# Joining the in-chunk products of a chunked scan: one pinned run for four chunks instead of one group for two

## Chip, cores and metric

The kernel runs on one core of a Trainium2 chip. The metric is the device time of one execution in microseconds (us). Engines: TensorE (PE, with its weight loads as PEld), VectorE (DVE), ScalarE (ACT), GpSimd (POOL) and SyncE (SP), which issues the DMAs here. Each engine works through its own row of instructions in order and waits at semaphores for the others.

## The reference

One layer of a hybrid backbone on 1024 latent and 128 context tokens (1152 rows, 1024 columns, f32). The change lies in the bidirectional Mamba-2 scan. With 128-token chunks, for each of 32 heads and for each direction:

```
L      = exp(where(mask, a_cs[i] - a_cs[j], -inf))
y_diag = (C B^T * L) @ x                      # inside a chunk
states = B^T (decay * x)                      # of each chunk
h      = dec * h + states                     # chain over the chunks
y_off  = C (exp(a_cs) * h_prev)               # from the chunks before
y      = y_f + flip(y_b) + D * x
```

Around it stand an input projection, a depthwise convolution with SiLU ahead of x, B and C, an output gate z, and a gated norm; behind it a gMLP branch, the merge, and a ConvFFN.

## The kernel before

The projection (names `gps`, L301 to L303) is written as 72 products of 128x384 per 128 output columns: three split-precision products for eight row blocks and three token blocks. Such a set of 72 is called a unit here. They fill TensorE's row between the small products of the scan. Their PSUM tiles have three buffers, and a unit's results go on through ACT (L356 to `pad` for x, B and C, L592 to `z`) before its next blocks can reuse a bank.

The scan works on 16 pairs of heads (q = 0 to 15), four pairs to a group that shares B and C. Chunks are taken in steps: s = 0 to 3 are two latent chunks each, s = 4 is the context chunk. For a pair:

- `ssd_loads(q, s)` (L632) loads R, the running sums broadcast for the decay matrix; for s < 4 E (tile EP), the exponents for the part from earlier chunks; for s = 4 H, the starting state.
- `mstage(s)` (L662) turns R into the masked decay matrix: biases on ACT (L672) and DVE (L674), a limit (L677), the exponentials on ACT (L678, and E's on L680), the product with C B^T (L688), and the sum of both directions, written back into R (L689).
- `chain(s)` (L697) carries the state on: weighted x (`xwf`, `xwb`, L694), products `pst` (L709, L710) in one PSUM bank, and steps of H on DVE (L713, L715).
- `ctx_state` (L717) makes the final context state in the same bank (`pstc`, L724).
- `main(s)` (L729) makes the output: the products `yo` (L740) with the state, the products `yd` (L744) inside the chunk, and on DVE L749 to L752 (L754 for the context). `yd` multiplies 128x64 halves: the two heads of a pair go to two halves of the array.

Steps are handed out between the units by `merge`. A scheduler then fixes each engine's row from its own model of time, with the scan's steps at a raised priority (P_SCAN). So the row of an engine isn't the order of the code, and the whole row may change where dependencies change. `queue_behind` (L274) is the way to pin one instruction directly after another in that order. At the end of a unit, `ptX` and `ptB` (L549) transpose x and B, after the convolution on DVE (L541, L542, L528).

Of the kernel before, what the change touches and what calls it, by code (L numbers as in the profile page):

```python
# [4 lines left out]
F32 = mybir.dt.float32  # L5
# [41 lines left out]
def gcol(t):  # L47
    return t if t < NL else t + 1
# [60 lines left out]
def body(tc, A, O):  # L109
# [517 lines left out]
    def cc_of(s):  # L627
        return [2 * s, 2 * s + 1] if s < 4 else [8]

    Rt, EPt, Ht = {}, {}, {}  # L630

    def ssd_loads(q, s):  # L632

        cc = cc_of(s)
        n = len(cc)
        R = spa.p.tile([128, 2, 2, 2, 128], F32, tag="R", name=f"R{q}{s}", bufs=3)
        if n == 2:
            SP.dma_start(R.rearrange("p d h c i -> p (d h) (c i)"),
                         acs_scr[q, :, :, cc[0]:cc[0] + 2].rearrange("d h c i -> (d h) (c i)").unsqueeze(0).to_broadcast([128, 4, 256]))
        else:  # L640
            SP.dma_start(R[:, :, :, 0, :].rearrange("p d h i -> p (d h) i"),
                         acs_scr[q, :, :, cc[0]].rearrange("d h i -> (d h) i").unsqueeze(0).to_broadcast([128, 4, 128]))
        Rt[q, s] = R
        if s < 4:
            E = spa.p.tile([128, 2, 2, 128], F32, tag="EP", name=f"EP{q}{s}", bufs=2)
            for h in range(2):
                SP.dma_start(E[64 * h:64 * h + 64].rearrange("p d c i -> p d (c i)"),
                             acs_scr[q, :, h, cc[0]:cc[0] + 2].rearrange("d c i -> d (c i)").unsqueeze(0).to_broadcast([64, 2, 256]))
            EPt[q, s] = E
        if s == 4:  # L650
            H = spa.p.tile([128, 8, 2, 128], F32, tag="H", name=f"H{q}", bufs=2)
            SP.dma_start(H[:, 0], A["h0"][q])
            Ht[q] = H

    def ssd(q):

        g = q // 4
        _, Bt, CT, CB = groups[g]
        X, Xt = xq[q]
        Dc = par[:, P_D + q:P_D + q + 1]  # L660

        def mstage(s):  # L662
            cc = cc_of(s)
            n = len(cc)
            R = Rt[q, s]
            for d in range(2):
                for h in range(2):
                    col = 32 * d + 2 * q + h
                    for i, c in enumerate(cc):
                        r = R[:, d, h, i, :]  # L670
                        if 4 * d + 2 * h + i < NACT:
                            S.activation(r, r, AF.Identity, bias=nb[:, c, col:col + 1])  # L672
                        else:
                            V.tensor_scalar(r, r, nb[:, c, col:col + 1], 60.0, op0=ALU.add, op1=ALU.min)  # L674
            Rv = R.rearrange("p d h c i -> p (d h) c i")[:, :, :n]
            if NACT:
                V.tensor_scalar(Rv[:, :NACT // 2], Rv[:, :NACT // 2], 60.0, None, op0=ALU.min)  # L677
            S.activation(Rv, Rv, AF.Exp)  # L678
            if s < 4:
                S.activation(EPt[q, s], EPt[q, s], AF.Exp)  # L680
            for d in range(2):
                if n == 2:
                    r = R[:, d].rearrange("p h c i -> p h (c i)")
                    cb = CB[:, d, cc[0]:cc[0] + 2, :].rearrange("p c i -> p (c i)").unsqueeze(1).to_broadcast([128, 2, 256])
                else:
                    r = R[:, d, :, 0, :]
                    cb = CB[:, d, cc[0], :].unsqueeze(1).to_broadcast([128, 2, 128])
                V.tensor_tensor(r, r, cb, op=ALU.mult)  # L688
            V.tensor_tensor(R[:, 0, :, :n], R[:, 0, :, :n], R[:, 1, :, :n], op=ALU.add)  # L689

        def xw(c0, n, d, dst):

            wv = wst[:, c0:c0 + n, 32 * d + 2 * q:32 * d + 2 * q + 2].unsqueeze(3).to_broadcast([128, n, 2, 64])
            V.tensor_tensor(dst.rearrange("p c (h e) -> p c h e", h=2), Xt[:, c0:c0 + n].rearrange("p c (h e) -> p c h e", h=2),  # L694
                            wv, op=ALU.mult)

        def chain(s):  # L697

            H = Ht[q]
            ks = [2 * s, 2 * s + 1] if s < 3 else [6]  # L700
            n = len(ks)
            x0 = spa.p.tile([128, 2, 128], F32, tag="xwf", name=f"xwf{q}{s}", bufs=2)[:, :n]
            x1 = spa.p.tile([128, 2, 128], F32, tag="xwb", name=f"xwb{q}{s}", bufs=2)[:, :n]
            xw(ks[0], n, 0, x0)
            cb0 = 7 - ks[-1]
            xw(cb0, n, 1, x1)
            ps = pst.tile([128, 2, 2, 128], F32, tag="st", name=f"pst{q}{s}")
            for i, k in enumerate(ks):
                PE.matmul(ps[:, i, 0, :], lhsT=Bt[:, k, :], rhs=x0[:, i, :], start=True, stop=True)  # L709
                PE.matmul(ps[:, i, 1, :], lhsT=Bt[:, 7 - k, :], rhs=x1[:, 7 - k - cb0, :], start=True, stop=True)  # L710
            for i, k in enumerate(ks):
                cd = cdk[:, k, :, 2 * q:2 * q + 2].unsqueeze(3).to_broadcast([128, 2, 2, 64])
                V.tensor_tensor(H[:, k + 1].rearrange("p d (h e) -> p d h e", h=2), H[:, k].rearrange("p d (h e) -> p d h e", h=2),  # L713
                                cd, op=ALU.mult)
                V.tensor_tensor(H[:, k + 1], H[:, k + 1], ps[:, i], op=ALU.add)  # L715

        def ctx_state():  # L717
            x0 = spa.p.tile([128, 2, 128], F32, tag="xwf", name=f"xwc{q}", bufs=2)
            for d in range(2):
                xw(8, 1, d, x0[:, d:d + 1])  # L720
            ps = pst.tile([128, 2, 2, 128], F32, tag="st", name=f"pstc{q}")
            so = spa.p.tile([128, 2, 128], F32, tag="so", name=f"so{q}")
            for d in range(2):
                PE.matmul(ps[:, 0, d, :], lhsT=x0[:, d, :], rhs=Bt[:, 8, :], start=True, stop=True)  # L724
            S.copy(so, ps[:, 0])
            for d in range(2):
                SP.dma_start(O[2 + d][0, 0, 2 * q:2 * q + 2].rearrange("h p n -> (h p) n"), so[:, d, :])

        def main(s):  # L729
            cc = cc_of(s)  # L730
            n = len(cc)
            R = Rt.pop((q, s))
            o = gcol(128 * cc[0])
            if s < 4:
                H = Ht[q]
                yo = pyo.tile([128, 2, 2, 128], F32, tag="yo", name=f"yo{q}{s}")
                for i, c in enumerate(cc):
                    for d in range(2):
                        k = c if d == 0 else 7 - c
                        PE.matmul(yo[:, d, i, :], lhsT=H[:, k, d, :], rhs=CT[:, 128 * c:128 * c + 128], start=True, stop=True)  # L740
            yd = pyd.tile([128, 512], F32, tag="yd", name=f"yd{q}{s}")[:, :128 * n]
            for i, c in enumerate(cc):
                for h in range(2):
                    PE.matmul(yd[64 * h:64 * h + 64, 128 * i:128 * i + 128], lhsT=Xt[:, c, 64 * h:64 * h + 64],  # L744
                              rhs=R[:, 0, h, i, :], start=True, stop=True, tile_position=(0, 64 * h))
            xv = X[:, o:o + 128 * n]
            if s < 4:
                E = EPt.pop((q, s))
                V.tensor_tensor(E, E, yo, op=ALU.mult)  # L749
                V.scalar_tensor_tensor(xv, xv, Dc, E[:, 0].rearrange("p c i -> p (c i)"), op0=ALU.mult, op1=ALU.add)  # L750
                V.tensor_tensor(xv, xv, E[:, 1].rearrange("p c i -> p (c i)"), op=ALU.add)
                V.tensor_tensor(xv, xv, yd, op=ALU.add)  # L752
            else:
                V.scalar_tensor_tensor(xv, xv, Dc, yd, op0=ALU.mult, op1=ALU.add)  # L754

        def nxt(s):
            if q + 1 < 16:
                ssd_loads(q + 1, s)

        def step(*fs):  # L760
            def run():
                for f, *a in fs:
                    f(*a)
            return run
        pro = [step((mstage, 4), (chain, 0)), step((mstage, 0), (chain, 1)), step((chain, 2)), step((chain, 3))]
        outs = [step((mstage, 1), (main, 4), (ssd_loads, q, 2)), step((mstage, 2), (main, 0), (ssd_loads, q, 3), (ctx_state,)),
                step((mstage, 3), (main, 1), (nxt, 4)), step((main, 2), (nxt, 0)), step((main, 3), (nxt, 1))]
        return pro, outs

    def merge(fills, steps):  # L770
# [35 lines left out]
    gtp.p, gtp.bufs = spa.p, 1  # L806
    run_unit(first_x)
    for s in (4, 0, 1):
        ssd_loads(0, s)
    after = None  # L810
    for q in range(17):
        steps = []
# [523 lines left out]
```

## Time and profile before

| what | value |
|---|---|
| median of 3 runs | 2480.05 us (2478.02 to 2480.44) |
| the profiled execution | 2481.27 us |
| its span | 2479.3 us |
| granted TensorE clock, mean | 0.994 |
| PE / DVE / ACT busy, share of the span | 98% / 75% / 45% |
| scan, first `yo` to last DVE step | about 134 to 958 us of the span |

Busy times count an instruction from its start to its end. Matmuls overlap, so the distance between two starts tells more than a duration. A line of the timeline gives start, duration, engine, line, operation, the tiles as out<-in, the shape, how many instructions were merged, and in brackets the idle time ahead of it with what ended it. One f32 product shows as two passes, a `gps` product as one.

### The profile page before, as it was taken

The numbers are of one execution on the slowest core, as the hardware profiler recorded it, in microseconds if no ns is written. First come the engines' busy times: TensorE is split into PE (matmuls) and PEld (weight loads), VectorE is DVE, ScalarE is ACT, GpSimd is POOL, SyncE is SP. The second block draws the span as 40 slices with busy tenths as digits, with TensorE's granted clock in tenths as the row PEclk, the third lists the DMA queues.
The fourth block names the chain that finished last, engine by engine and source line by source line (L and its number), as shares of the span: only waits on it lengthen the run. The fifth ranks groups of instructions, "written<-read, shape, count | busy, mean of one in ns | idle before, by whom it ended". The sixth has DMA issues, their size and how long they took to land.

```text
span 2479.3 us, 37397 instructions
## 1 busy us (share of the span) xinstructions
PE 2428.8 (98%) x13951; PEld 2271.1 (92%) x13951; DVE 1854.7 (75%) x3150; ACT 1110.4 (45%) x2118; POOL 27.0 (1%) x82
## 2 busy tenths in 40 slices
PE   7989999999999998999999999999999999999998
PEld 5989999999999897899999998999999999998877
DVE  5668988878868886963546757559999989998554
ACT  5545655555555553211345545354433333344443
POOL 0000000000000000000000000000000000000000
PEclk9999999999999999999999999999999999999999
DMA  6134334433433445731456657542222221224674
GB/s 257 39 98 148 119 126 140 134 95 115 140 100 104 142 127 185 229 104 63 133 163 201 214 158 245 156 138 77 75 65 71 68 69 60 67 64 132 217 244 133
DMA packets 204181, 323.21 MB, mean 130 GB/s; under 512 B 19328, under 2 KB 113312, under 8 KB 203872
## 3 DMA queue, kind: packets, MB, share of 16 engines
q1 hardware_dynamic: 204000, 320.82, 40.7%
q8 instruction: 110, 1.80, 0.3%
q14 instruction: 71, 0.58, 0.1%
HBM read 278.22 MB, written 42.52 MB: 129 GB/s over the span
## 4 chain that ended last, share of the span: by engine, by line
PE 89%; DMA 5%; DVE 3%; ACT 1%; issue 1%; SPq 1%; POOL 0%; DVEq 0%; POOLq 0%; ACTq 0%
PE gps L301 10%; PE gps L302 10%; PE gps L303 10%; PE pup L302 7%; PE pup L301 7%; PE pup L303 7%; PE fo L1152 4%; PE fo L1154 4%; PE fo L1153 4%; PE pbs L301 2%; PE pbs L303 2%; PE pbs L302 2%; PE yo L740 2%; PE yd L744 2%; DMA R<-acs_scr 2%; PE pv L865 1%
## 5 line engine op out<-in xcount | busy, mean ns | idle before, releaser
L85 DVE TENSOR_TENSOR wl<-wr,wh 128x512 fp32r<-128x512 f32 x544 | 372.0, 690 | 254.7 <-ACT wh L84 242.4
L84 ACT CAST wh<-wr 128x512 fp32r<-128x512 f32 x544 | 333.8, 619 | 473.8 <-PE pup L302 121.6
L301 PE MATMUL gps<-hh,wh 128*128 128x384 f32 x1512 | 518.6, 343 | 0.2 <-ACT pad L356 0.2
L303 PE MATMUL gps<-hh,wl 128*128 128x384 f32 x1512 | 514.1, 340 | 0.0
L302 PE MATMUL gps<-hl,wh 128*128 128x384 f32 x1512 | 513.6, 340 | 0.0
L1140 DVE SCALAR_TENSOR_TENSOR acc<-U,fpar,acc 128x960 f32<-128x960 f32 (+1 forms) x352 | 444.3, 1267 | 16.0 <-ACT acc L1133 8.2
L302 PE MATMUL pup<-h2l,wh 128*128 128x384 f32 x1056 | 353.1, 334 | 0.0
L301 PE MATMUL pup<-h2h,wh 128*128 128x384 f32 x1056 | 352.9, 334 | 0.0
L303 PE MATMUL pup<-h2h,wl 128*128 128x384 f32 x1056 | 352.4, 334 | 0.0
L301 PEld LDWEIGHTS gps<-hh,wh 128*128 128x128 f32 x1512 | 285.0, 188 | 6.4 <-issue 5.5
L302 PEld LDWEIGHTS gps<-hl,wh 128*128 128x128 f32 x1512 | 285.0, 189 | 3.9 <-issue 3.8
L303 PEld LDWEIGHTS gps<-hh,wl 128*128 128x128 f32 x1512 | 284.7, 188 | 4.1 <-issue 4.1
L301 PEld LDWEIGHTS pup<-h2h,wh 128*128 128x128 f32 x1056 | 198.2, 188 | 1.3
L302 PEld LDWEIGHTS pup<-h2l,wh 128*128 128x128 f32 x1056 | 198.2, 188 | 1.3
L303 PEld LDWEIGHTS pup<-h2h,wl 128*128 128x128 f32 x1056 | 198.2, 188 | 0.0
L1122 ACT COPY U<-pup 128x384 f32<-128x384 f32 (+1 forms) x132 | 58.5, 443 | 225.0 <-PE pup L303 225.0
L672 ACT ACTIVATE R<-R,nb 128x128 f32<-128x128 f32 x288 | 93.1, 391 | 137.9 <-DMA R<-acs_scr 131.3
L1152 PE MATMUL fo<-wh,gh 128*128 128x512 f32 x384 | 148.0, 396 | 0.4 <-ACT wh L84 0.4
L1153 PE MATMUL fo<-wh,gl 128*128 128x512 f32 x384 | 148.3, 396 | 0.0
L1154 PE MATMUL fo<-wl,gh 128*128 128x512 f32 x384 | 139.9, 396 | 0.0
L301 PE MATMUL pbs<-ysh,wh 128*128 128x384 f32 x384 | 129.6, 338 | 3.2 <-ACT wh L84 1.7
L303 PE MATMUL pbs<-ysh,wl 128*128 128x384 f32 x384 | 129.8, 338 | 0.1
(303 smaller groups left out, 3966.9 us busy)
## 6 DMA issues: line engine op xcount, KB each, us to landing
wr<-in_w_dn SPq DMA_DIRECT2D x132, 256.0 KB, 2.8
wr<-in_w_in SPq DMA_DIRECT2D x130, 256.0 KB, 2.8
R<-acs_scr SPq DMA_DIRECT2D x64, 512.0 KB, 4.4
wr<-in_w_bs SPq DMA_DIRECT2D x96, 256.0 KB, 3.5
wr<-in_w_up SPq DMA_DIRECT2D x90, 256.0 KB, 2.6
EP<-acs_scr SPq DMA_DIRECT2D x128, 128.0 KB, 3.2
wmt<-in_w_modt SPq DMA_DIRECT2D x32, 512.0 KB, 3.8
wr<-in_w_bu SPq DMA_DIRECT2D x48, 256.0 KB, 3.0
```

Of the source, the lines that this page charges most:

```text
L84: self.nc.scalar.copy(hi, w)
L85: self.nc.vector.tensor_tensor(lo, w, hi.bitcast(F32), op=ALU.subtract)
L301: PE.matmul(ps, lhsT=wh, rhs=xh, start=first and k == 0, stop=False)
L302: PE.matmul(ps, lhsT=wh, rhs=xl, start=False, stop=False)
L303: PE.matmul(ps, lhsT=wl, rhs=xh, start=False, stop=last and k == n - 1)
L672: S.activation(r, r, AF.Identity, bias=nb[:, c, col:col + 1])
L740: PE.matmul(yo[:, d, i, :], lhsT=H[:, k, d, :], rhs=CT[:, 128 * c:128 * c + 128], start=True, stop=True)
L1122: S.copy(u[:, a // 64:b // 64, 1:65], src.rearrange("p (r c) -> p r c", c=64))
L1140: tap = V.scalar_tensor_tensor(av[:, r0:r1], u[:, r0 + dy - 1:r1 + dy - 1, dx:dx + 64], w[i], av[:, r0:r1], op0=ALU.mult, op1=ALU.add)
L1152: PE.matmul(outs[c][h], lhsT=mh[:, cs_], rhs=wh, start=k == 0, stop=False)
L1153: PE.matmul(outs[c][h], lhsT=ml[:, cs_], rhs=wh, start=False, stop=False)
L1154: PE.matmul(outs[c][h], lhsT=mh[:, cs_], rhs=wl, start=False, stop=k == NFF - 1)
```

## The change

The products inside chunks leave `main`. A new function `within(b)` does them for four latent chunks at once (b = 0 with step 1's outputs, b = 1 with step 3's, the latter with the context chunk too). It pins the eight (or ten) products one behind the other with `queue_behind`, and adds one bank of 512 columns to X in one DVE instruction in place of two of 256 columns. The summed decay matrices no longer overwrite R: they go to tiles of their own (RS for four chunks, RSc for the context chunk), so R is free after the sum. The context chunk's product is written to the unused half of the `pstc` bank. The loads are split into `load_R`, `load_E`, `load_H`; E of steps 2 and 3 is loaded later, after `main(0)` and `main(1)`, and its exponential moves from `mstage` to `main`. The rest of the steps keep their places in the code.

```diff
@@ loads @@
-    def ssd_loads(q, s):
+    def load_R(q, s):
...
         Rt[q, s] = R
-        if s < 4:
-            E = spa.p.tile([128, 2, 2, 128], F32, tag="EP", name=f"EP{q}{s}", bufs=2)
...
+    def load_E(q, s):
+
+        cc = cc_of(s)
+        E = spa.p.tile([128, 2, 2, 128], F32, tag="EP", name=f"EP{q}{s}", bufs=2)
...
+    def load_H(q):
+        H = spa.p.tile([128, 8, 2, 128], F32, tag="H", name=f"H{q}", bufs=2)
...
@@ mstage @@
-            R = Rt[q, s]
+            R = Rt.pop((q, s))
+            if s == 4:
+                RS[2] = spa.p.tile([128, 2, 1, 128], F32, tag="RSc", name=f"RSc{q}", bufs=2)
+            elif s % 2 == 0:
+                RS[s // 2] = spa.p.tile([128, 2, 4, 128], F32, tag="RS", name=f"RS{q}{s}", bufs=2)
+            sum_ = RS[s // 2][:, :, 2 * (s % 2):2 * (s % 2) + n]
...
             if s < 4:
-                S.activation(EPt[q, s], EPt[q, s], AF.Exp)
+                exp_E(s)
...
-            V.tensor_tensor(R[:, 0, :, :n], R[:, 0, :, :n], R[:, 1, :, :n], op=ALU.add)
+            V.tensor_tensor(sum_, R[:, 0, :, :n], R[:, 1, :, :n], op=ALU.add)
+
+        def exp_E(s):
+            if s < 2:
+                S.activation(EPt[q, s], EPt[q, s], AF.Exp)
@@ ctx_state @@
+            RS[3] = ps[:, 1, 0, :]
@@ main @@
...
+            xv = X[:, o:o + 256]
+            E = EPt.pop((q, s))
+            if s >= 2:
+                S.activation(E, E, AF.Exp)
+            V.tensor_tensor(E, E, yo, op=ALU.mult)
+            V.scalar_tensor_tensor(xv, xv, Dc, E[:, 0].rearrange("p c i -> p (c i)"), op0=ALU.mult, op1=ALU.add)
+            V.tensor_tensor(xv, xv, E[:, 1].rearrange("p c i -> p (c i)"), op=ALU.add)
+
+        def within(b):
+
+            yd = pyd.tile([128, 512], F32, tag="yd", name=f"yd{q}{b}")
+            todo = [(yd[:, 128 * i:128 * i + 128], 4 * b + i, RS[b][:, :, i]) for i in (2, 3, 0, 1)]
+            if b == 1:
+                yc = RS[3]
+                todo.append((yc, 8, RS[2][:, :, 0]))
+            first = None
+            for p, c, r in todo:
                 for h in range(2):
-                    PE.matmul(yd[64 * h:64 * h + 64, 128 * i:128 * i + 128], lhsT=Xt[:, c, 64 * h:64 * h + 64],
-                              rhs=R[:, 0, h, i, :], start=True, stop=True, tile_position=(0, 64 * h))
...
+                    m = PE.matmul(p[64 * h:64 * h + 64], lhsT=Xt[:, c, 64 * h:64 * h + 64], rhs=r[:, h, :],
+                                  start=True, stop=True, tile_position=(0, 64 * h))
+                    if first is not None:
+                        queue_behind(m, first)
+                    first = m
+            xv = X[:, 512 * b:512 * b + 512]
+            V.tensor_tensor(xv, xv, yd, op=ALU.add)
+            if b == 1:
+                xv = X[:, gcol(NL):gcol(NL) + 128]
+                V.scalar_tensor_tensor(xv, xv, Dc, yc, op0=ALU.mult, op1=ALU.add)
@@ steps @@
-        outs = [step((mstage, 1), (main, 4), (ssd_loads, q, 2)), step((mstage, 2), (main, 0), (ssd_loads, q, 3), (ctx_state,)),
-                step((mstage, 3), (main, 1), (nxt, 4)), step((main, 2), (nxt, 0)), step((main, 3), (nxt, 1))]
+        outs = [step((mstage, 1), (load_R, q, 2)), step((mstage, 2), (main, 0), (load_R, q, 3), (load_E, q, 2), (ctx_state,)),
+                step((mstage, 3), (main, 1), (within, 0), (load_E, q, 3), (nxt, load_R, 4), (nxt, load_H)),
+                step((main, 2), (nxt, load_R, 0), (nxt, load_E, 0)), step((main, 3), (within, 1), (nxt, load_R, 1), (nxt, load_E, 1))]
```

Three places in the engines' rows show what the scheduler makes of this. In them the lines of the changed kernel are other numbers: `yo` is L752, `yd` L771, `pst` L722 and L723, the `pstc` products L737, the R product L697, the sum L698, the state steps L726 and L728, the weighted x L707, the bias L683, the limit L686; `ptX` keeps L549.

First place: TensorE, pair 7, before. The four `yd` products of one step:

```order
L740 MATMUL yo_5042<-CT_2908,H_4506 128x128
L744 MATMUL yd_5047<-R_4561,Xtok_4541 64x128
L301 MATMUL gps<-hh,wh_4888 128x384
L744 MATMUL yd_5047<-R_4561,Xtok_4541 64x128
L302 MATMUL gps<-hl,wh_4888 128x384
L709 MATMUL pst_4831<-xwf_4827,Btok_2751 128x128
L710 MATMUL pst_4831<-xwb_4828,Btok_2751 128x128
L744 MATMUL yd_5047<-R_4561,Xtok_4541 64x128
L303 MATMUL gps<-hh,wl_4889 128x384
L744 MATMUL yd_5047<-R_4561,Xtok_4541 64x128
```

The same pair's first `within` after the change, on TensorE:

```order
L549 MATMUL ptB_5117<-cst,BT_4938 128x128
L771 MATMUL yd_5180<-RS_4706,Xtok_4524 64x128 x8
L303 MATMUL gps<-hh,wl_5223 128x384
L301 MATMUL gps<-hh,wh_5314 128x384
L302 MATMUL gps<-hl,wh_5314 128x384
```

The products of a step stood apart, with `gps` and `pst` between them; now eight stand together. In the whole program 109 such runs become 38.

Second place: TensorE ahead of the transposes of pair 4's X, before (`wh_2713` and `wl_2714` are weights of a unit):

```order
L302 MATMUL gps<-hl,wh_2713 128x384
L303 MATMUL gps<-hh,wl_2714 128x384
L301 MATMUL gps<-hh,wh_2713 128x384
L302 MATMUL gps<-hl,wh_2713 128x384
L303 MATMUL gps<-hh,wl_2714 128x384
L301 MATMUL gps<-hh,wh_2713 128x384
L740 MATMUL yo_2340<-CT_775,H_1781 128x128 x4
L549 MATMUL ptX_2779<-cst,X_2629 128x128 x3
```

and after the change, from pair 2's first `within` on:

```order
L771 MATMUL yd_2275<-RS_1991,Xtok_1809 64x128 x8
L722 MATMUL pst_2010<-xwf_2006,Btok_744 128x128
L723 MATMUL pst_2010<-xwb_2007,Btok_744 128x128
L722 MATMUL pst_2010<-xwf_2006,Btok_744 128x128
L723 MATMUL pst_2010<-xwb_2007,Btok_744 128x128
L722 MATMUL pst_2057<-xwf_2053,Btok_744 128x128
L723 MATMUL pst_2057<-xwb_2054,Btok_744 128x128
L722 MATMUL pst_2057<-xwf_2053,Btok_744 128x128
L723 MATMUL pst_2057<-xwb_2054,Btok_744 128x128
L549 MATMUL ptX_2768<-cst,X_2625 128x128 x3
L549 MATMUL ptX_2805<-cst,X_2625 128x128 x3
L301 MATMUL gps<-hh,wh_2798 128x384
```

The `gps` products that stood ahead of the transposes are gone from here; they stand earlier. Between two sets of four `pst` nothing is left. Part of what VectorE has in its row at that place, after the change:

```order
L683 TENSOR_SCALAR R_2731<-R_2731,nb 128x128 x4
L85 TENSOR_TENSOR wl_3024<-wr_2802,wh_3023 128x512
L686 TENSOR_SCALAR R_2731<-R_2731 128x512
L697 TENSOR_TENSOR R_2340<-R_2340,CB_985 128x512 x2
L728 TENSOR_TENSOR H_1774<-H_1774,pst_1944 128x256
L599 TENSOR_TENSOR ssq<-ssq,z_2298 128x1152
L697 TENSOR_TENSOR R_2404<-R_2404,CB_985 128x512 x2
L698 TENSOR_TENSOR RS_2507<-R_2340 128x2x256
L726 TENSOR_TENSOR H_1774<-H_1774,cdk 128x256
L697 TENSOR_TENSOR R_2731<-R_2731,CB_985 128x512 x2
```

The state steps of one bank (`pst_1944`) and the next (`pst_2010`, further down) stand among the decay matrices of two pairs and the gate's norm.

Third place: TensorE at the end of the scan, before (pair 15's last step), and after it:

```order
L301 MATMUL gps<-hh,wh_9525 128x384
L302 MATMUL gps<-hl,wh_9525 128x384
L744 MATMUL yd_9454<-R_9360,Xtok_8955 64x128 x4
L303 MATMUL gps<-hh,wl_9526 128x384
L301 MATMUL gps<-hh,wh_9525 128x384
L302 MATMUL gps<-hl,wh_9525 128x384
```

```order
L302 MATMUL gps<-hl,wh_9525 128x384
L303 MATMUL gps<-hh,wl_9526 128x384
L752 MATMUL yo_9311<-CT_7289,H_8887 128x128 x3
L737 MATMUL pstc_9327<-Btok_7138,xwc_9324 128x128 x2
L752 MATMUL yo_9347<-CT_7289,H_8887 128x128 x4
L752 MATMUL yo_9400<-CT_7289,H_8887 128x128 x4
L771 MATMUL yd_9418<-RS_9297,Xtok_8922 64x128 x8
L771 MATMUL pstc_9327<-RSc_9043,Xtok_8922 64x128 x2
L752 MATMUL yo_9409<-CT_7289,H_8887 128x128 x4
L895 MATMUL pv_9709<-vwh,hh 128x512
```

Before, `gps` products stand around each of pair 15's output steps, and 43 behind its last. After, all of them stand ahead, and the next stage (`pv`) follows the last `yo`. Pair 14's output steps look like this too.

More of the change, by code (lines that the diff above doesn't have):

```diff
@@ L630, in body @@
     Rt, EPt, Ht = {}, {}, {}
-    def ssd_loads(q, s):
+    def load_R(q, s):
         cc = cc_of(s)
-        n = len(cc)
         R = spa.p.tile([128, 2, 2, 2, 128], F32, tag="R", name=f"R{q}{s}", bufs=3)
-        if n == 2:
+        if len(cc) == 2:
             SP.dma_start(R.rearrange("p d h c i -> p (d h) (c i)"),
@@ L643, in ssd_loads @@
         Rt[q, s] = R
-        if s < 4:
-            E = spa.p.tile([128, 2, 2, 128], F32, tag="EP", name=f"EP{q}{s}", bufs=2)
[L646 to L653, printed above, removed]
+    def load_E(q, s):
+        cc = cc_of(s)
+        E = spa.p.tile([128, 2, 2, 128], F32, tag="EP", name=f"EP{q}{s}", bufs=2)
+        for h in range(2):
+            SP.dma_start(E[64 * h:64 * h + 64].rearrange("p d c i -> p d (c i)"),
+                         acs_scr[q, :, h, cc[0]:cc[0] + 2].rearrange("d c i -> d (c i)").unsqueeze(0).to_broadcast([64, 2, 256]))
+        EPt[q, s] = E
+    def load_H(q):
+        H = spa.p.tile([128, 8, 2, 128], F32, tag="H", name=f"H{q}", bufs=2)
+        SP.dma_start(H[:, 0], A["h0"][q])
+        Ht[q] = H
     def ssd(q):
@@ L660, in ssd @@
         Dc = par[:, P_D + q:P_D + q + 1]
+        RS = {}
         def mstage(s):
@@ L727, in ctx_state @@
                 SP.dma_start(O[2 + d][0, 0, 2 * q:2 * q + 2].rearrange("h p n -> (h p) n"), so[:, d, :])
+            RS[3] = ps[:, 1, 0, :]
         def main(s):
             cc = cc_of(s)
[L731 to L740, printed above, removed]
@@ L741, in main @@
-            yd = pyd.tile([128, 512], F32, tag="yd", name=f"yd{q}{s}")[:, :128 * n]
-            for i, c in enumerate(cc):
-                for h in range(2):
-                    PE.matmul(yd[64 * h:64 * h + 64, 128 * i:128 * i + 128], lhsT=Xt[:, c, 64 * h:64 * h + 64],
-                              rhs=R[:, 0, h, i, :], start=True, stop=True, tile_position=(0, 64 * h))
[L746 to L754, printed above, removed]
@@ L756, in nxt @@
-        def nxt(s):
+            o = 128 * cc[0]
+            H = Ht[q]
+            yo = pyo.tile([128, 2, 2, 128], F32, tag="yo", name=f"yo{q}{s}")
+            for i, c in enumerate(cc):
+                for d in range(2):
+                    k = c if d == 0 else 7 - c
+                    PE.matmul(yo[:, d, i, :], lhsT=H[:, k, d, :], rhs=CT[:, 128 * c:128 * c + 128], start=True, stop=True)
+            xv = X[:, o:o + 256]
+            E = EPt.pop((q, s))
+            if s >= 2:
+                S.activation(E, E, AF.Exp)
@@ L757, in nxt @@
+        def nxt(f, *a):
             if q + 1 < 16:
-                ssd_loads(q + 1, s)
+                f(q + 1, *a)
         def step(*fs):
@@ L808, in body @@
     for s in (4, 0, 1):
-        ssd_loads(0, s)
+        load_R(0, s)
+        if s < 4:
+            load_E(0, s)
+    load_H(0)
     after = None
```

## Prediction

> **What bounds the kernel now.** I read the busy times first, then the stretch in which the changed code runs (150 to 955 us), then PE's waits there. Each `windows` row gives, behind the stretch, busy us and instruction count of PE, PEld, DVE, ACT, POOL, then PEclk, DMA share and GB/s.
>
> ```profile
> PE 2428.8 (98%) x13951; PEld 2271.1 (92%) x13951; DVE 1854.7 (75%) x3150; ACT 1110.4 (45%) x2118; POOL 27.0 (1%) x82
> ```
> ```profile
> 150.00:955.00 805.00, 800.38 (x5190) 756.67 (x5189) 659.16 (x1470) 434.61 (x842) 3.90 (x36) 1.00 0.39 121
> ```
> ```profile
> PE pst L710 <- DVE xwb L694: 1.7, 1, 1.7
> PE yo L740 <- DVE EP L749: 1.1, 2, 0.9
> ```
>
> PE is busy 800.38 of 805 us, and its two longest sums of waits are 1.7 and 1.1 us. So TensorE's own work is the time today; DVE, with 659.16 us, runs 18% below it. Whoever takes work from PE gains it, but only while DVE keeps up at every single place.
>
> **What the change takes from PE.** A run of `yd` products (128x64 array halves) costs more than its passes. The timeline of PE (start, duration, then what) shows a run of two chunks, and runs of one product alone:
>
> ```profile
> 283.25 0.34 PE L303 MATMUL gps<-hh,wl 128*128 128x384 f32 x1
> 283.52 0.66 PE L744 MATMUL yd<-R,Xtok 128*64 128x128 f32 x8
> 284.10 0.44 PE L301 MATMUL gps<-hh,wh 128*128 128x384 f32 x1
> 284.39 0.34 PE L302 MATMUL gps<-hl,wh 128*128 128x384 f32 x1
> 284.56 0.34 PE L303 MATMUL gps<-hh,wl 128*128 128x384 f32 x1
> 284.74 0.33 PE L301 MATMUL gps<-hh,wh 128*128 128x384 f32 x1
> ```
> ```profile
> 528.21 0.43 PE L744 MATMUL yd<-R,Xtok 128*64 128x128 f32 x2
> 528.58 0.44 PE L301 MATMUL gps<-hh,wh 128*128 128x384 f32 x1
> 528.95 0.43 PE L744 MATMUL yd<-R,Xtok 128*64 128x128 f32 x2
> ```
> ```profile
> 195.79 0.89 PE yo L740 x8
> ```
>
> Undisturbed `gps` steps take (284.74 - 284.39)/2 = 0.175 us. From 283.25 to 284.39 stand two of them and the run of two chunks: 1.14 - 0.35 = 0.79 us. From 528.21 to 528.95 stand one of them and one product alone: 0.74 - 0.175 = 0.566 us; I price a lone product like a chunk, since its partner half stays empty. So a chunk is 0.79 - 0.566 = 0.226 us and a run has 0.340 us on top. The order has 109 runs before (53 of four products, 3 of three, 14 of two, 39 of one: 165 chunk slots) and 38 runs after (32, of which six are cut in two: 149 slots). Taken off: 71 x 0.340 + 16 x 0.226 = 24.1 + 3.6 = **27.7 us**.
>
> **What it adds: places where PE has nothing else in its row.** Engines work their rows in order, and the new order bunches the `gps` products ahead of some scan steps. What decides there is DVE's row. Its groups of 150 to 955 us:
>
> ```profile
> L688 DVE TENSOR_TENSOR R<-R,CB 128x512 f32<-128x512 f32 x124 | 80.3, 687 | 12.3 <-ACT R L678 12.3
> L85 DVE TENSOR_TENSOR wl<-wr,wh 128x512 fp32r<-128x512 f32 x92 | 63.0, 687 | 10.3 <-ACT wh L84 9.9
> L674 DVE TENSOR_SCALAR R<-R,nb 128x128 f32<-128x128 f32 x278 | 62.9, 282 | 51.1 <-DMA R<-acs_scr 50.6
> L715 DVE TENSOR_TENSOR H<-H,pst 128x256 f32<-128x256 f32 x112 | 46.6, 416 | 0.2
> L713 DVE TENSOR_TENSOR H<-H,cdk 128x256 f32<-128x256 f32 x110 | 45.9, 420 | 0.3
> L749 DVE TENSOR_TENSOR EP<-EP,yo 128x512 f32<-128x512 f32 x64 | 43.7, 683 | 25.2 <-PE yo L740 23.0 <-DMA wr<-in_w_in 2.1
> L689 DVE TENSOR_TENSOR R<-R 128x512 f32<-128x512 f32 x63 | 43.3, 687 | 0.2
> L750 DVE SCALAR_TENSOR_TENSOR X<-X,par,EP 128x256 f32<-128x256 f32 x64 | 30.8, 482 | 0.8
> L751 DVE TENSOR_TENSOR X<-X,EP 128x256 f32<-128x256 f32 x64 | 26.9, 421 | 0.6
> L752 DVE TENSOR_TENSOR X<-X,yd 128x256 f32<-128x256 f32 x64 | 26.7, 416 | 4.9 <-PE yd L744 4.4
> L677 DVE TENSOR_SCALAR R<-R 128x512 f32<-128x512 f32 x62 | 26.2, 423 | 2.2 <-ACT R L672 1.5
> L528 DVE SCALAR_TENSOR_TENSOR z<-pad,z 128x1152 f32<-128x1152 f32 x16 | 21.6, 1353 | 1.2 <-ACT pad L527 1.2
> L599 DVE TENSOR_TENSOR ssq<-ssq,z 128x1152 f32<-128x1152 f32 x15 | 20.3, 1355 | 0.2 <-ACT z L598 0.2
> L541 DVE SCALAR_TENSOR_TENSOR X<-pad,par,X 128x1153 f32<-128x1153 f32 x14 | 19.9, 1419 | 2.1 <-ACT X L540 2.1
> L542 DVE SCALAR_TENSOR_TENSOR X<-pad,par,X 128x1153 f32<-128x1153 f32 x14 | 19.9, 1418 | 0.1
> ```
> ```profile
> 286.80 0.87 DVE L674 TENSOR_SCALAR R<-R,nb 128x128 f32<-128x128 f32 x4
> ```
> ```profile
> 262.00:289.00 27.00, 27.00 (x190) 25.80 (x189) 23.61 (x51) 13.57 (x26) 0.10 (x1) 1.00 0.38 112
> ```
>
> Four L674 in a row take 0.87, not 4 x 0.282 = 1.13 us: neighbours overlap by 0.085. *Place A*: PE's transposes `ptX` of pair 4's X stand ahead of all further `gps`, and need DVE's last convolution step (L528). From DVE's product with pair 1's last `yo`, which PE itself must have delivered, to that step stand 57 DVE instructions: 18 biases L674; 8 L688 and 2 L689; 2 L85; 9 state steps L713/L715; 5 L677 (one half as wide); 4 L694 (priced as L713, two of them half as wide at 0.29); one each of L749, L750, L751, L597 (1.22, estimated between L750 and L599 by its 1024 columns), L599, L541, L542, L528; and the new add of 512 columns of `yd`, not in the trace: between 0.416 (L752, half as wide) and 0.687 (L689, as wide in SBUF), taken as L749's 0.683, which reads PSUM too. Sum 29.5, less 57 x 0.085: 24.7 us back to back. PE's own row holds only 17 `gps`, 3 `ptX`, 13 `pst`/`yo` of two passes (0.89/8 = 0.111 each) and a run of four chunks in it: 3.0 + 0.3 + 2.9 + 1.2 = 7.4 us. In the order of before 155 `gps`, 27 us, stand between the same two points.
>
> No DVE stretch is fully packed. The densest kind (262 to 289 us, above) took 27.00/23.61 = 1.14 of its busy time, the scan's mean is 805/659.16 = 1.22. I take 1.18; the ends are 1.00 and 1.22. PE then idles 29.1 - 7.4 = 21.7 us at A (17.3 to 22.7). *B* and *C* are the same piece one and two groups later (pairs 8 and 12) with 97 and 59 `gps` on PE, 21.3 and 14.7 us: idle 7.8 (3.4 to 8.8) and 14.4 (10.0 to 15.4). *D1*: pair 14's second state step waits for 30 DVE instructions, 10.9 us, against 5.8 of PE: 7.1 (5.1 to 7.5).
>
> *D2 and E*: in the last two pairs the out steps stand without one `gps` between them. The scan's exponent E of steps 2 and 3 is now taken in the step itself, behind a load that starts only when an earlier step has freed its buffer:
>
> ```profile
> EP<-acs_scr SPq DMA_DIRECT2D x128, 128.0 KB, 3.2
> ```
> ```profile
> 946.81 0.61 ACT L680 ACTIVATE EP<-EP 128x512 f32<-128x512 f32 x1
> 949.15 0.31 ACT L598 ACTIVATE z<-X 128x128 f32<-128x128 f32 x1 [1.73 <-DVE X L597]
> 955.09 1.06 ACT L598 ACTIVATE z<-X 128x1024 f32<-128x1024 f32 x1 [5.63 <-DVE X L597]
> 956.18 1.27 ACT L600 ACTIVATE X<-X,par 128x1153 f32<-128x1153 f32 x1
> 957.35 0.84 ACT L610 COPY gt<-gps 128x384 f32<-128x384 f32 x2
> 958.08 1.15 ACT L84 CAST vwh<-wr 128x512 fp32r<-128x512 f32 x2
> ```
>
> D2 (pair 14): 30 DVE instructions, 13.7 us x 1.18, and ACT's square (1.06) before the next `gps` bank is free: 17.2, less 8.5 of PE: 8.7 (6.3 to 9.3). E (pair 15): first `yo` 0.67; step 0 (L749 to L751) 1.59; load 3.2 and exponent 0.61; steps 2 and 3, 3.18; last add 0.68; L597 1.22; then ACT from 955.09 to the first cast's end at about 958.7, 3.6: 14.7, less 5.2 of PE: 9.5. Before, 68 `gps` stood among pair 15's out steps and 43 behind them.
>
> Sum: 21.7 + 7.8 + 14.4 + 7.1 + 8.7 + 9.5 = 69.2 us lost (51.6 to 73.2), 27.7 gained: **+41.5** (+23.9 to +45.5). Against the profiled run (2481.27 us, span 2479.3) that is 2522.8; the median of before lies 1.2 lower, so **2522 us**.
>
> **Costs taken as nothing.** The summed matrices go to tiles of their own: same add, and the R tile is free earlier; DVE's 50.6 us of waiting for R can only shrink, which PE does not feel where it is ahead. The context product moves into the `st` bank and holds it until its DVE step; in the order `ptX` or `gps` cover that in most pairs. Uncovered it is a 0.35 us step and two hand-offs, at most 1 us x 16. Splitting the loads moves E and H behind R on SP's queue; nothing is added. On ACT the late exponent waits for E's load, with weight casts and the next biases queued behind it; in the middle of the scan `gps` on PE hides that, at the end it is priced in E.
>
> [...]
>
> **Rivals.**
> - *PE stays the limit*: 2481.3 - 27.7 - 1.2 = 2452 us. For it: 99.4% busy, hardly a wait today. Against: place A needs 24.7 us of DVE even with no gap while PE holds 7.4. It decides only if the DVE pieces took under a third of their sums. Chance 0.07.
> - *Even*: waits near 28 us, as if only A, or only D and E, showed: 2480. Every bound above is beyond that. 0.05.
> - *Worse*: the held `st` bank and the late exponent show in every pair, 1 us x 16 and more: 2538 to 2555. Against: `gps` stand around most of these steps. 0.10.
> - That the runs are not joined is excluded by the order (38 for 109).
>
> **How the numbers follow.** Forecast 0.78, rivals as given. The forecast's bounds are 2504 to 2526; with the worse case's nearer part and as much below, the range is 2500 to 2550. What a measurement can tell from no change is about 0.2%, 5 us: faster 0.08, same 0.05, slower 0.87.
>
> **What would show it.** PE waits of 15 us and more ahead of `pst` and `ptX` near 270 to 290 us, smaller ones near 500 and 725, none with the `yd` runs; PE in the last two pairs alternating with DVE; `yd` runs of 16 passes at 0.11 us each two; the part behind the scan shifted, not longer. Wrong would be PE still above 98% of the scan (first rival), or waits in every pair (third).

## The result, and the profile after

| | median us | runs | ratio to before (95%) |
|---|---|---|---|
| before | 2480.24 | 4 (2478.02 to 2480.97) | |
| after | 2533.94 | 4 (2530.94 to 2535.26) | 1.0215 (1.0204 to 1.0227) |

The change costs 53.7 us. The prediction had 2522 us, bounds of 2504 to 2526 around it, and a range of 2500 to 2550. The profiled execution of the changed kernel took 2535.06 us, its span 2533.3. The first rows answer those of before: the busy times of the page, and a row of the windows for the stretch of the scan, 53 us longer than before (busy us and count of PE, PEld, DVE, ACT, POOL, then PEclk, DMA share, GB/s).

```profile
PE 2421.9 (96%) x13951; PEld 2288.0 (90%) x13951; DVE 1857.8 (73%) x3118; ACT 1111.5 (44%) x2118; POOL 26.1 (1%) x82
```
```profile
150.00:1008.00 858.00, 796.07 (x5222) 776.04 (x5220) 662.16 (x1438) 435.62 (x841) 3.57 (x36) 0.96 0.37 113
```

PE was busy 99.4% of this stretch before and is 92.8% now, and its mean granted clock fell from 1.00 to 0.96. The waits of PE from 150 to 1025 us (total, times, longest):

```profile
PE pst L722 <- DVE H L728: 39.5, 5, 12.2
PE pv L895 <- ACT vwh L84: 7.8, 1, 7.8
PE yd L771 <- DVE X L777: 5.9, 5, 2.2
PE yo L752 <- DVE EP L757: 4.8, 6, 1.3
PE gps L301 <- ACT z L592: 4.1, 2, 2.5
```

The largest, 39.5 us in five waits, is that of the state products for H. The timeline of PE shows two of the five at place A (idle time and releaser in brackets):

```profile
267.69 1.09 PE L771 MATMUL yd<-RS,Xtok 128*64 128x128 f32 x16 [0.62 <-DVE X L777]
275.50 0.76 PE L722 MATMUL pst<-xwf,Btok 128*128 128x128 f32 x2 [6.71 <-DVE H L728]
...
286.49 0.77 PE L722 MATMUL pst<-xwf,Btok 128*128 128x128 f32 x2 [8.95 <-DVE H L728]
...
289.21 1.54 PE L549 MATMUL ptX<-cst,X 128*128 128x128 f32 x6 [0.67 <-DVE X L528]
290.40 0.67 PE L301 MATMUL gps<-hh,wh 128*128 128x384 f32 x1
290.87 0.52 PE L302 MATMUL gps<-hl,wh 128*128 128x384 f32 x1
...
294.07 0.52 PE L303 MATMUL gps<-hh,wl 128*128 128x384 f32 x1
...
295.17 0.33 PE L302 MATMUL gps<-hl,wh 128*128 128x384 f32 x1
295.34 0.33 PE L303 MATMUL gps<-hh,wl 128*128 128x384 f32 x1
```

The waits stand where the prediction put them. The last rows hold what it didn't have: from 290.87 to 294.07 a `gps` product takes 0.320 us (3.20 us for ten), from 295.17 on 0.17 us as ever. The window rows around it say why:

```profile
270.00:275.00 5.00, 0.00 (x0) 0.00 (x0) 5.00 (x13) 4.38 (x9) 0.00 (x0) 0.56 0.34 92
...
290.00:295.00 5.00, 5.00 (x20) 5.00 (x19) 4.25 (x6) 1.90 (x5) 0.00 (x0) 0.55 0.00 0
295.00:300.00 5.00, 5.00 (x32) 5.00 (x32) 2.36 (x4) 1.60 (x2) 0.10 (x1) 1.00 0.01 3
```

While PE waits here, its clock goes to half (1.00 in the window from 269 to 270 us, 0.50 in each window of 1 us from 271 to 294 us), and it stays there for 5.3 us after the work is back at 289.21 us: PE is busy for all of 290 to 295 us, but this row counts 20 products where the next 5 us have 32.

So the scan's time has three parts. From 150 us to the first `prs` product behind the scan (969.20 us of the span before, 1022.60 after) I add up, in windows of 5 us, PE's busy time; what is not busy is idle, busy time times (1 - PEclk) counts as lost to the clock, and the rest is PE's work at full clock. The rows just shown are three of the 175 of the changed kernel. For all kernels of this study:

| kernel | runs (chunk slots) | pairs ahead | 150 us to `prs` | work | idle | clock | median us |
|---|---|---|---|---|---|---|---|
| before | 109 (165) | 13 | 819.2 | 812.5 | 6.7 | 0.0 | 2480.24 |
| after | 38 (149) | 0 | 872.6 | 785.2 | 67.5 | 19.9 | 2533.94 |
| e1 product in the `yd` bank | 80 (164) | 13 | 823.1 | 804.8 | 11.1 | 7.2 | 2477.76 |
| e2 product not pinned | 69 (157) | 14 | 832.1 | 796.1 | 29.4 | 6.7 | 2494.50 |
| e3 before, with the hold | 63 (144) | 0 | 901.8 | 793.7 | 86.4 | 21.7 | 2564.60 |
| e4 before, late place only | 107 (163) | 13 | 830.9 | 815.2 | 15.2 | 0.5 | 2484.80 |
| e5 early exponents | 38 (149) | 0 | 869.8 | 783.9 | 65.8 | 20.1 | 2531.16 |
| e6 before, priority 400 | 81 (145) | 13 | 798.4 | 794.2 | 4.2 | 0.0 | 2461.61 |
| e7 as e1, priority 400 | 53 (148) | 13 | 801.1 | 789.2 | 8.8 | 3.0 | 2458.25 |
| e8 as e7, two gates moved | 52 (146) | 13 | 798.4 | 787.4 | 6.9 | 4.2 | 2455.54 |
| e9 second `st` bank | 104 (185) | 12 | 832.2 | 816.7 | 8.6 | 6.8 | 2494.51 |
| e10 as e9, priority 400 | 37 (148) | 10 | 810.0 | 790.7 | 16.1 | 3.2 | 2474.02 |
| e11 as e6, two gates moved | 81 (145) | 13 | 796.0 | 795.2 | 0.8 | 0.0 | 2460.06 |
| e12 as e6, second `st` bank | 80 (144) | 6 | 813.6 | 800.6 | 11.3 | 1.7 | 2482.86 |

Runs and slots are those of the `yd` products, counted as in the prediction. "Pairs ahead" counts, in PE's row as built, how many of the 15 later pairs have their first state step ahead of the last `yo` of the pair before; where it is 0 the idle time is 65 us and more, elsewhere under 30. Between before and after: work -27.3, idle +60.8, clock +19.9, together +53.4 us, which is the 1022.60 - 969.20 us by which the part behind the scan is shifted. That part itself is as long as before (1510.1 and 1510.7 us).

### The profile page after: what moved, and what is told of

Read it like the earlier page. It is cut to its first block, busy times and chain, and to the rows that moved or that the text cites. A ratio compares the mean times of both kernels' runs of the same rounds, so it can differ in the third digit from the quotient of the medians.

```text
span 2533.3 us, 37303 instructions
## 1 busy us (share of the span) xinstructions
PE 2421.9 (96%) x13951; PEld 2288.0 (90%) x13951; DVE 1857.8 (73%) x3118; ACT 1111.5 (44%) x2118; POOL 26.1 (1%) x82
## 4 chain that ended last, share of the span: by engine, by line
PE 83%; DMA 7%; DVE 5%; ACT 3%; issue 1%; SPq 1%; POOL 0%; DVEq 0%; ACTq 0%; POOLq 0%
PE gps L301 10%; PE gps L303 10%; PE gps L302 10%; PE pup L302 7%; PE pup L301 7%; PE pup L303 7%; PE fo L1182 3%; PE fo L1184 3%; PE fo L1183 3%; PE yo L752 2%; PE pbs L301 2%; PE pbs L303 2%; PE pbs L302 2%; DMA R<-acs_scr 2%; DMA wr<-in_w_bs 1%; PE pv L895 1%
## 5 line engine op out<-in xcount | busy, mean ns | idle before, releaser
L302 PE MATMUL pbs<-ysl,wh 128*128 128x384 f32 x384 | 129.1, 336 | 0.0
```

The lines of the kernel that those rows point to most:

```text
L302: PE.matmul(ps, lhsT=wh, rhs=xl, start=False, stop=False)
```

## The experiments

**The suspicion.** The prediction took the order as given. But why are the `gps` used up ahead of the state steps, when state steps of pair 2 stood among pair 1's outputs before? The timeline of PE before, with the rows of `gps` and `yd` left out:

```profile
228.46 0.38 PE L709 MATMUL pst<-xwf,Btok 128*128 128x128 f32 x2
228.68 0.39 PE L710 MATMUL pst<-xwb,Btok 128*128 128x128 f32 x2
228.90 1.06 PE L740 MATMUL yo<-CT,H 128*128 128x128 f32 x8
...
229.79 0.39 PE L709 MATMUL pst<-xwf,Btok 128*128 128x128 f32 x2
```

and of the changed kernel, at the end of pair 14:

```profile
963.61 1.16 PE L752 MATMUL yo<-CT,H 128*128 128x128 f32 x8 [0.78 <-DVE EP L757]
965.31 1.09 PE L771 MATMUL yd<-RS,Xtok 128*64 128x128 f32 x16 [0.54 <-DVE X L777]
966.24 0.39 PE L771 MATMUL pstc<-RSc,Xtok 128*64 128x128 f32 x4
967.92 1.16 PE L752 MATMUL yo<-CT,H 128*128 128x128 f32 x8 [1.29 <-DVE EP L757]
969.78 0.49 PE L722 MATMUL pst<-xwf,Btok 128*128 128x128 f32 x2 [0.70 <-DVE X L780]
```

Here the state step of pair 15 waits for L780, the DVE step that reads the context product: the two share the only `st` bank. The product is the last of the pinned run of `within(1)`, so the bank, taken at `ctx_state` in the second of five out steps, comes free only when the pair's last run is through. No state step of the next pair can stand ahead of that, and in the changed kernel none does (0 of 15, 13 before). The theory, "held bank": this hold makes the loss. The rival, "joined runs": a run of four chunks needs two decay stages, comes late by itself, and uses up the cover.

**e1 to e4: bank, pin, hold alone, late place alone.** e1 puts the product into a bank that it doesn't keep:

```diff
-            RS[3] = ps[:, 1, 0, :]
...
-                yc = RS[3]
+                yc = pyd.tile([128, 512], F32, tag="yd", name=f"yc{q}")[:, :128]
```

> The changed kernel with one edit: the context chunk's product goes to a tile of its own in the yd bank, as before the change, and no longer into the other half of the st bank; the pinned order of the ten products stays. Theory 'held bank': the product stands at the end of the pinned run, so the only st bank is kept from ctx_state until a pair's last out step, the next pair's state steps cannot start before, gps products are used up ahead of them, and PE then waits for DVE at A to E. Without the hold the waits fall from 72 to under 20 us in the scan and the time comes back to 2470 to 2490 us. Rival 'joined runs': runs of four chunks come late by themselves (each needs two decay stages), so the gps are used up all the same; 2525 to 2535 us, waits at A to E as in the changed kernel.

Measured: 2477.76 us, ratio 0.9992 (0.9981 to 1.0003). The whole loss is gone, with `within` still there and 24 of its 32 runs of sixteen passes still whole. PE's waits from 150 to 975 us:

```profile
PE gps L301 <- ACT z L592: 2.9, 1, 2.9
PE prs L878 <- DMA wsT<-in_sgu_w: 2.7, 1, 2.7
PE yo L751 <- DVE EP L756: 2.5, 1, 2.5
...
PE pst L722 <- DVE H L728: 0.8, 1, 0.8
```

The 39.5 us of `pst` for H are down to one wait of 0.8. There is a second thing to see: the runs are 80, not 38. `queue_behind` keeps the order of the ten products, but lets other instructions in between. All 16 context products now stand apart from their runs: they wait for the DVE step on the one `yd` bank, and `gps` go in ahead of them. Eight of the 32 runs are cut as well, four of them into lone products. That the runs of the changed kernel are whole also because nothing of the next pair may stand there is likely, but no run here shows it.

e2 takes only the pin from the context product:

```diff
-                    if first is not None:
+                    if first is not None and c < 8:
                         queue_behind(m, first)
```

> The changed kernel with one edit: the two products of the context chunk are not pinned behind the eight others; they stay in the st bank. Held bank: they can run as soon as their own decay matrix is there, which is the first one made, so the bank is free early in most pairs; about half of the loss goes, 2490 to 2510 us, and the waits at B and C (500 and 725 us) vanish. Joined runs: nothing but a few more runs, 2530 to 2545 us.

Measured: 2494.50 us, 1.0058 (1.0038 to 1.0077). Of the 53.7 us, 39 go with this one condition. Idle time is 29.4 us, and the waits at 500 and 725 us are gone as expected; those near A and at the end stay (150 to 1100 us):

```profile
PE pv L895 <- ACT vwh L84: 14.6, 2, 9.0
PE pst L722 <- DVE H L728: 14.2, 3, 8.2
```

e3 is the kernel before with the hold alone. RS[3] is the free half of the bank as in the change, RS[4] the last `yd` product of `main(3)`; the summed matrix of the context chunk has its own small tile here too:

```diff
...
+        def context():
+            yc = RS[3]
+            for h in range(2):
+                m = PE.matmul(yc[64 * h:64 * h + 64], lhsT=Xt[:, 8, 64 * h:64 * h + 64], rhs=RS[2][:, h, 0, :],
+                              start=True, stop=True, tile_position=(0, 64 * h))
+                queue_behind(m, RS[4])
+            xv = X[:, gcol(NL):gcol(NL) + 128]
+            V.scalar_tensor_tensor(xv, xv, Dc, yc, op0=ALU.mult, op1=ALU.add)
...
-        outs = [step((mstage, 1), (main, 4), (ssd_loads, q, 2)), step((mstage, 2), (main, 0), (ssd_loads, q, 3), (ctx_state,)),
-                step((mstage, 3), (main, 1), (nxt, 4)), step((main, 2), (nxt, 0)), step((main, 3), (nxt, 1))]
+        outs = [step((mstage, 1), (ssd_loads, q, 2)), step((mstage, 2), (main, 0), (ssd_loads, q, 3), (ctx_state,)),
+                step((mstage, 3), (main, 1), (nxt, 4)), step((main, 2), (nxt, 0)), step((main, 3), (context,), (nxt, 1))]
```

e4 is the control: the same, but with a tile of its own that isn't held:

```diff
-            yc = RS[3]
+            yc = pyd.tile([128, 512], F32, tag="yd", name=f"ydc{q}")[:, :128]
```

> The kernel before with the hold alone: the context chunk's product is written into the st bank behind the state of the context, pinned behind the last product of the pair's last out step; its summed decay matrix has a small tile of its own. Runs stay as they are (two chunks at most, three at a pair's end), the exponent and the loads too. Held bank: this alone makes the loss, without any joined run: 2530 to 2570 us, PE waits ahead of pst near 270, 510, 730 us and in the last two pairs. Joined runs: 2478 to 2486 us.

> As the run before, with the context chunk's product at the same late place and pinned alike, but in a yd tile of its own instead of the st bank: the control for the move. Held bank: 2476 to 2486 us, no waits at A to E. If it were the late place and not the bank, 2530 us and more as with the bank.

Measured: e3 2564.60 us, 1.0339 (1.0320 to 1.0358); e4 2484.80 us, 1.0014 (1.0001 to 1.0026). Without one joined step, the hold makes the kernel 3.4% slower, more than the change itself. I had expected the runs to stay as they were; e3 has 63 of them, nearly all of two or three chunks. PE's waits in e3, 150 to 1055 us:

```profile
PE pst L713 <- DVE H L719: 49.2, 7, 8.6
PE yo L745 <- DVE EP L754: 9.9, 9, 2.7
PE yd L749 <- ACT X L600: 7.0, 1, 7.0
```

The wait of `pst` for H is there again, and the late place alone costs 0.14%, some 4 us. The two kernels differ in the bank alone. The loss needs no joined step (e3), and goes while most joined runs are still whole (e1), which speaks against the rival "joined runs"; e10 below has nearly all of them joined.

**e5: the late exponents**, back in `mstage` with their earlier loads:

```diff
-            if s < 2:
+            if s < 4:
                 S.activation(EPt[q, s], EPt[q, s], AF.Exp)
...
```

> The changed kernel with the exponents of E for steps 2 and 3, and their loads, back where they stood before the change (in the decay stages, ahead of the steps). Theory 'held bank': nothing changes, 2530 to 2538 us, the waits at A to E stay. Rival 'late exponent' (term E of the prediction has 3.8 us of load and exponent in it, and the third rival lets it show in every pair): 4 to 20 us faster, 2514 to 2530 us, above all at the end of pair 15.

Measured: 2531.16 us, 1.0221 (1.0201 to 1.0241), not to be told from the changed kernel. The waits are the same, the one at pair 15's end to the digit:

```profile
PE pst L722 <- DVE H L728: 39.1, 5, 12.2
PE pv L893 <- ACT vwh L84: 7.8, 1, 7.8
```

So the 3.8 us of load and exponent in term E weren't part of it.

**e6 to e8: keeping runs whole without a hold.** e6 is the kernel before with `P_SCAN` 400 for 50; e7 is e1 with it; e8 is e7 with `NGATE[12:]` 1, 0, 0, 1, 1 for 1, 1, 1, 0, 0.

> The kernel before with one number changed: scan steps take priority by 400 instead of 50 places. The order then cuts the runs of products less often, 81 in the scan instead of 109, with no joined steps and no held bank. If a run costs 0.340 us beside its passes, as the prediction has it, 28 x 0.340 = 9.5 us go: 2469 to 2474 us. If the cost lies in the passes alone: 2479 to 2483 us.

> The joined runs without the hold (context chunk's product in a tile of its own in the yd bank), with the priority of 400 as in the run before: 53 runs in the scan. By 0.340 us for each of 56 runs less and 13 chunk slots by 0.226 us: 22 us, less some 10 us of waits that stay near 220 and 260 us in the order: 2462 to 2472 us. If joining as such costs cover, it is no faster than the run before it.

> As the run before, with two gate units moved from rounds 13 and 14 to rounds 15 and 16, so that gps products stand among the last pairs' out steps. If the end of the scan still lacks cover, 3 to 5 us less than the run before, 2458 to 2468 us; if not, the same.

Measured: e6 2461.61 us, 0.9935 (0.9918 to 0.9951); e7 2458.25 us, 0.9923 (0.9907 to 0.9940); e8 2455.54 us, 0.9912 (0.9897 to 0.9927). All three beat both kernels, and all by more than expected. For e6 I had left out of the expectation that most runs that vanish are lone products, which also pair up: 145 chunk slots for 165. With them 28 x 0.340 + 20 x 0.226 = 14.0 us, and PE's work fell by 18.3. A window row of e8 shows PE at 99% again:

```profile
150.00:935.00 785.00, 778.12 (x5182) 756.65 (x5182) 656.27 (x1439) 433.51 (x844) 4.53 (x36) 0.99 0.40 123
```

That e8 is ahead of e7 by its gates can't be said: the intervals overlap.

**e9, e10 and e12: a second `st` bank.** e9 and e10 have product, pin and hold as the change has them, e10 with the priority of 400 too; e12 is the kernel before with that priority. All three make this trade of banks:

```diff
-    g_cm, pg = pool("pg", bufs=3, space=PSUM)
+    g_cm, pg = pool("pg", bufs=2, space=PSUM)
...
-    st_cm, pst = pool("pst", space=PSUM)
+    st_cm, pst = pool("pst", bufs=2, space=PSUM)
...
```

> The changed kernel, product and pins untouched, with a second st bank, taken from the three banks of gps (two are left; at the start the third block's sum uses the new st bank). Held bank: a second bank lets the next pair's state steps start while the product still holds the first, so the waits at A to E go: under 15 us of waits in the scan, 2478 to 2500 us, the rest being runs cut again and the gps bank given away. If the hold cost by something else than the bank (the pin, the late place), 2525 us and more.

> As the run before, with the scan's priority at 400: 39 runs in the scan, about as few as in the changed kernel, with the cover kept. By 70 runs of 0.340 us and 16 chunk slots of 0.226 us less than before, 27 us, less a few us of waits and up to 8 us for the gps bank given away behind the scan: 2455 to 2468 us. If joined runs cost cover themselves, 2480 us and more.

> The control for the two runs with a second st bank: the kernel before, priority 400, three gps banks cut to two and a second st bank, no joined step. If the given-away gps bank is what kept the joined kernel with two st banks at 2474.0 us, this one is slower than the same kernel with three gps banks (2461.6 us) by about as much as 2474.0 lies above its forecast: 2468 to 2480 us. If the bank costs nothing, 2458 to 2464 us, and the miss lies in the joined runs.

Measured: e9 2494.51 us, 1.0060 (1.0044 to 1.0077); e10 2474.02 us, 0.9981 (0.9971 to 0.9992); e12 2482.86 us, 1.0015 (1.0006 to 1.0025). In e9, from 150 to 985 us, the waits for H are gone but for 0.4 us with the hold in place, which confirms the bank from the other side, though its runs are cut up (104):

```profile
PE gps L301 <- ACT pad L356: 3.6, 2, 1.9
PE prs L879 <- DMA wsT<-in_sgu_w: 2.3, 1, 2.3
PE yo L752 <- DVE EP L757: 2.3, 1, 2.3
PE pst L722 <- DVE H L728: 0.4, 1, 0.4
```

e10 has 37 runs (39 were expected), one fewer than the changed kernel, with the pin and the hold in place, and idles 16.1 us where that one idles 67.5: with another bank and the higher priority, runs of four chunks don't use up the cover. This and e3 leave nothing of the rival "joined runs". e10 missed its range by 6 us. e12 says where they went: the same trade of banks costs the kernel before 21 us at this priority (2461.61 to 2482.86), where I had allowed for 8; e12 itself lies 3 us above the range that I gave it. Beside e12, the joined steps of e10 are worth some 8 us where both have two `st` banks (ratios 0.9981 and 1.0015).

**e11: what the joining itself is worth**, with priority and gates as in e8 and no joined step.

> The kernel before with priority 400 and the two gate units moved to rounds 15 and 16, no joined step: what is left for the joining itself. If a joined step is worth its runs (28 fewer than here: 9 us) the kernel is 3 to 9 us behind the joined one with the same priority and gates (2455.5 us): 2458 to 2465 us; if joining gives back what it takes, they are level, 2453 to 2458 us.

Measured: 2460.06 us, 0.9918 (0.9901 to 0.9936), beside e8's 0.9912 (0.9897 to 0.9927). It lies in the range of "worth its runs", but the intervals overlap, so it stays open whether joining is worth 4 us or nothing. The parts show how little is left: work falls by 7.8 us from e11 to e8, idle time rises by 6.1 and the loss to the clock by 4.2. The scan of e8 is thus 2.4 us longer than that of e11, so in the profiled runs whatever e8 gains lies behind the scan.

## Why the prediction was right, and where it wasn't

- **The limit and the gain: right.** A run was priced at 0.340 us and a chunk at 0.226: 27.7 us off. PE's work fell by 27.3. Over the table's other orders the same two prices, times the runs and slots gone, give the change of work within 4.3 us in all but e10 (28.3 by the prices, 21.8 measured).
- **The places: right, in sum somewhat too dear.** Gaps of over 0.5 us in PE's row, forecast and found: A 21.7 and 17.0; B 7.8 and 5.8; C 14.4 and 13.2; D1 7.1 and 8.7; D2 8.7 and 8.6; E 9.5 and 10.5. Sum 69.2 and 63.8; less the idle time that before had too, the difference of the two kernels is 60.8. At A, DVE's row from the product with pair 1's last `yo` to the end of the convolution took 26.4 us, 1.07 times its sum of 24.7 and not 1.18 times.
- **A term was missing: the clock.** 19.9 us. The sum had PE go on at full speed after each wait; it was 69.2 - 27.7 = 41.5, and the runs gave 60.8 - 27.3 + 19.9 = 53.4. The forecast of 2522 lies 12 us low for this: without it the idle time priced too dear would have brought the time to 8 us below the forecast. Errors of opposite sign partly cancelled, which is luck. The 2533.94 us lie above the forecast's own upper bound of 2526, and within the stated range only as this was widened for the third rival.
- **The step that failed: "at most 1 us x 16" for the held bank.** It was listed among the costs taken as nothing, and let stand in the third rival as a hand-off in every pair. Its own hand-offs are small indeed (0.70 us in the row at 969.78). Its price is in the order: the hold keeps the next pair's state steps out of the pair's outputs, and that is what empties the places A to E. I had read this emptiness off the order and priced it, and so came near the total, but named nothing in the change as its cause beyond the late load at E, and took the bank for nearly free. Without the finished order to read from, at most 16 us of cost against 27.7 of gain would have made the change a faster one. e1, e3, e9 and e10 show that it is the bank.
- **Rivals.** "PE stays the limit" (2452 us) didn't come, and e1 without the hold isn't there either, at 2477.76 us and 80 runs; e8, with the higher priority, is near it at 2455.54. "Even" didn't come. "Worse" (2538 to 2555 us) was missed by 4 us, but its mechanism, a cost of 1 us and more in every pair, isn't what the waits show: 39.5 of the 67.5 us are five waits.
- **Late exponent, RS tiles, loads.** The late exponent costs nothing that can be measured (e5), also not at E. The RS tiles and the order of loads were not tried by themselves; e1 has both and no loss.
- **What would show it.** As said: waits of 15.7 us ahead of `pst` at 270 to 290, smaller ones near 500 and 725 (though the one at 725 was the longest single one, 12.2), PE and DVE in turn in the last two pairs, runs of 16 passes in 1.09 us where one of eight took 0.66 (0.11 for each two more), the part behind the scan shifted and not longer. Not as said: no waits with the `yd` runs were forecast, and there are five of them for DVE's add, 5.9 us in all.

## What to carry to other kernels

Where a change parks a result in the free half of a bank that another chain of work uses, the price isn't the hand-off but everything of that chain which may no longer go ahead; ask for each shared buffer who is next in it and how far ahead of now that one used to run. Pinning instructions behind one another sets their order and not that they stand together; to have a run whole, everything that it reads must be ready, and a higher priority for it (in e6 one number, 0.65% faster than before) did more here. A wait of the engine that sets the time should be priced with the slow stretch behind it (in e1, 2.2 us on top of a wait of 2.89 us).

## What the runs showed of the chip

That PE's waits cost more than their length was not expected. In windows of 2 us, the granted clock in the scans is 1.00 or 0.50 but for the windows at the edges (in the changed kernel 0.66 from 270 to 272 us and 0.87 from 294 to 296 us). In the scan of before, from 150 us on, the longest gap is 1.75 us, and no window is below 0.98; ahead of that, at a gap of 4.21 us from 136.84 on, the clock goes to half until 148.2 us. In e1, this wait was enough:

```profile
226.03 0.39 PE L723 MATMUL pst<-xwb,Btok 128*128 128x128 f32 x2
229.31 0.69 PE L301 MATMUL gps<-hh,wh 128*128 128x384 f32 x1 [2.89 <-ACT z L592]
229.79 0.53 PE L302 MATMUL gps<-hl,wh 128*128 128x384 f32 x1
...
234.59 0.53 PE L302 MATMUL gps<-hl,wh 128*128 128x384 f32 x1
...
235.39 0.34 PE L302 MATMUL gps<-hl,wh 128*128 128x384 f32 x1
```

After 2.89 us without work, 15 `gps` products from 229.79 to 234.59 take 4.80 us, 0.32 us each, where 0.175 is usual: the wait costs 2.2 us beyond its length. In the scans of before, after, e1, e2, e4 and e6 to e12, from 150 us on, of the gaps from 1.7 to 2.5 us some were followed by such a stretch (1.70 and 2.05 us in e10, 1.90 in e9, 2.49 in e1) and some weren't (1.70 in e9, 1.75 before, 2.44 in e10); every longer one in a scan was (from 2.55 us in the changed kernel and 2.89 in e1 up to 12.15 in the changed kernel), while one of 2.74 us just behind the scan of e6 wasn't. The stretches at half clock lasted 3.41 us after the 1.70 us in e10, 6.83 in e1, 10.24 after the 1.90 us in e9, and 23.89, 6.83, 17.07, 10.24, 6.83, 3.41 and 10.24 us in the scan of the changed kernel: each 3.41 us or a whole multiple of it. So the gap of 1.90 us in e9 had a longer stretch behind it than the 2.89 us in e1. What starts a stretch, and what sets its length, no run here shows.
